# Four retention gates of a hybrid decoder, computed as one block product of seven, with the gate applied at the bank

## The chip, the core and the metric

The kernel runs on one core of one Trainium2 chip. The time is that of one execution on the device in microseconds (us); of several runs the median is taken. A profile is one further execution, recorded instruction by instruction.

The engines are named as in the profile: PE is TensorE (matmuls; PEld its weight loads), DVE is VectorE, ACT is ScalarE, POOL is GpSimd, SP is SyncE. The last two mostly start transfers here.

## What is computed

Two decoder layers over 512 tokens with 1024 channels, fp32, and a final norm. Of a layer, the part that matters:

```
h = rmsnorm(x);  z = h @ w_in        # q, k, v of attention | rq rk rv rg of retention | gate_a | gate_b
ya = sliding_window_sink_attention(aq, ak, av, sinks) @ w_a
r  = chunkwise_retention(rq, rk, rv)                        # 4 heads, 256 values each
r  = r * rsqrt(mean(r*r, axis=-1) + EPS)                    # per head
r  = r * silu(rg)                                           # rg: 1024 columns of z
yb = r @ w_b
x  = x + (sigmoid(ga) * ya + sigmoid(gb) * yb) @ w_out
x  = x + square(relu(rmsnorm(x) @ w_up)) @ w_down
```

## The kernel before

**Layout.** Activations lie with channels on the 128 partitions and tokens along the row: a tile of 128 x 512 is 128 channels of all tokens, and x is eight of these. The 1024 columns of rg are thus eight tiles `rg[0]` to `rg[7]`, two for each retention head.

**Precision.** Every fp32 operand is split into a high and a low part of a narrower kind (`split`: ScalarE writes the high part, VectorE the rest), and each product is three matmuls: high by high, high by low, low by high (`products`, lines 390 to 392).

**Weights.** `unit_order` lists all weight units, 128 x 1024 floats (512 KB) each. SyncE loads them in that order into five `raw` buffers; `split_until` splits them (line 338 on ScalarE, line 339 on VectorE) into four `hi` and four `lo` buffers, up to four units ahead of their use.

**Chunks.** `chunk("w_in", ...)` makes one tile of 128 output channels from one unit: 8 blocks of input channels by 3, so 24 matmuls with 512 columns into one of five banks of the pool `ps_mm`; a function then evacuates the bank. The retention gates come from `put_rg(i)` (line 981): times the row of inverse norms, and for i >= 4 at once `silu(i)`. The merge gate of `gate_b` comes from `gate(...)` (line 826) in tiles `gb`.

**Block products of seven.** The values of retention (`values`), the output projection (`output`) and most of the MLP multiply two-by-two blocks with seven block products instead of eight. One operand's sums are made in DRAM by GpSimd's transfers (`sum_steps`, tensors `sums_*`) and by `add_values` on VectorE (line 318); the other operand's are made on the core. For `values` these are `Turned`: the upper and lower halves of the input channels by the first and second half of the tokens (256 each). `load` fetches two `xg` tiles of x again by GpSimd's queue (line 878), `build` scales them (line 888), forms the four differences (lines 891 to 894) and splits them. `turned[1]` to `turned[4]` are the results, each four blocks of 128 x 256; `quarter(half, tokens)` gives the plain ones out of `xh`, `xl`.

**Order.** The program is traced in the order below; a scheduler then fixes each engine's queue ahead of time by a priority that follows this order and by its own estimate of when each instruction can run, so later matmuls may be pulled forward where earlier ones wait. `background` generators (attention, retention) are advanced from within chunks; `drain()` runs them to their end.

1. q, k, v of attention; eight chunks of gate_a, `qk(0)`, rg chunks 0 to 3, with attention behind them; `drain()`
2. sigmoids of gate_a, `silu` of 0 to 3, `qk(1)`, `turned.build(0)` after attention's last split, `turned.load(2)`
3. rg chunks 4 and 5
4. `w_a`: four units, eight results of 12 matmuls, each multiplied into gate_a (line 1142); `turned.build(2)` after the second unit
5. `values(turned)`, then retention of heads 0 and 1 behind `qk(2)`, `qk(3)`
6. rg chunks 6 and 7, then gate_b chunks 0 to 3, with retention of heads 2 and 3 behind them
7. `w_b` results 0 to 3 (`group`), gate_b chunks 4 to 7, `w_b` results 4 to 7, the output projection `wo`

**Retention.** `Head.scores` makes a head's decayed scores (tile `ret`), `outputs(e)` its two output tiles (bank `r` of the pool `ps_aux`, three banks): ScalarE copies the bank to `rr` (line 1044) and squares it (line 1046). `norm` makes the inverse norms, and `finish` multiplies the gate by them (line 1066), by `rr` (line 1067) and splits the result for `w_b`.

**GpSimd's queue.** `pace(tile)` counts evacuations; every second one copies a mark of one column and then issues the next step of `sum_steps`, so the sums in DRAM are spread over the layer. Between `turned.take()` and the values' first evacuation `quiet` holds it.

Of the kernel before, what the change touches and what calls it, by code (L numbers as in the profile page):

```python
# [10 lines left out]
F32 = mybir.dt.float32  # L11
F32R = mybir.dt.float32r
AF = mybir.ActivationFunctionType
ALU = mybir.AluOpType
# [28 lines left out]

N_IN = 38
N_BLOCK = 8
# [11 lines left out]
def unit_order(layer):  # L57

    order = [("w_in", i) for i in range(4 + 2 + 8 + 2 + 4 + 2 + 2)]
    order += [("w_a", i) for i in range(4)]  # L60
    order += [("rv", part, u) for part in range(7) for u in range(2)]
    order += [("w_in", i) for i in range(24, 34)]
    order += [("w_b", i) for i in range(4)]
    order += [("w_in", i) for i in range(34, 38)]
# [50 lines left out]
@with_exitstack  # L115
def decoder(ctx, tc, xT, x_first, w_in, w_rv, w_a, w_b, w_wo, w_up, w_pair, w_down, w_end, tables, decay, band, g_last, out):
    nc = tc.nc
# [62 lines left out]
    def load_until(n):  # L180
# [26 lines left out]
    sums_last = dram.tile([P, 2, UNIT], F32, name="sums_last")  # L207
    MIXING = {"rv": w_rv, "wo": w_wo}
    sums_mix = {
        name: [dram.tile([2, P, 2 * UNIT], F32, name=f"sums_{name}{l}") for l in range(DEPTH)] for name in MIXING  # L210
    }
# [102 lines left out]
    def add_values(i):  # L314
        part = order[i][2]
        if part in (2, 4):
            raws[i] = raws.pop(i - 2)
            nc.vector.tensor_tensor(raws[i], raws[i], raws.pop(i - 4), ALU.add)

# [294 lines left out]
    def layer_body(layer):  # L614
# [366 lines left out]
        def put_rg(i):  # L981
            def put(ps):
                if i % 2 == 0:
                    two = big("z")
                    rg[i], rg_next[i + 1] = two[:, 0, :], two[:, 1, :]
                else:
                    rg[i] = rg_next.pop(i)
                nc.vector.tensor_tensor(rg[i], ps, rstd(), ALU.mult)
                if i >= 4:
                    pace(rg[i])  # L990
                    silu(i)

            return put

        def silu(i):
# [12 lines left out]
        class Head:  # L1008
# [5 lines left out]
            def scores(self, js):  # L1014
# [14 lines left out]
                if js[-1] == NB - 1:  # L1029
                    slots.give(*rq.pop(h), *rk.pop(h))  # L1030
                    self.rr, self.sq = [], []

            def outputs(self, e):
# [10 lines left out]
                nc.scalar.activation(r, ps, AF.Copy)  # L1044
# [33 lines left out]
        def retention(pair):  # L1078
# [47 lines left out]
        turned.load(2)  # L1126
        for i in (4, 5):
            chunk("w_in", layer, xs, put_rg(i))


# [17 lines left out]

        load_decay(0)
        values(turned)  # L1150
        background.append(retention(0))
# [12 lines left out]

        for c in range(4):
            gate_tile(c)
            chunk("w_in", layer, xs, gate(gates[c]))
# [45 lines left out]

        TOKENS = (slice(0, H), slice(H, T))
        ms = Mixed()
# [64 lines left out]
        def output():  # L1280
# [5 lines left out]
            def multiply(ps, moving, start=True):  # L1286
                for u in range(2):
                    hi, lo = unit("wo", layer)
                    for k in range(2):
                        vh, vl = moving[2 * u + k]  # L1290
                        for n in range(4):
# [3 lines left out]
                            for w, v in ((hi, vh), (hi, vl), (lo, vh)):  # L1295
# [7 lines left out]
                                ).ins  # L1303

            def both(t):
                return t.rearrange("p (a t) -> p a t", t=H)

# [498 lines left out]
def _w_in_units(w):  # L1806
# [19 lines left out]
    units += qk(1)  # L1826
    units += _units_chunks(w, O_RG + T + r(2 * P))
    units += qk(2) + qk(3)
    units += _units_chunks(w, O_RG + T + 2 * P + r(2 * P))
    units += _units_chunks(w, O_GB + r(D))  # L1830
# [11 lines left out]
def _mixing_blocks(w):  # L1842

    blocks = []
    for u in range(2):
# [4 lines left out]
        blocks.append(np.concatenate(parts, 1))  # L1850
    return blocks


# [43 lines left out]
def _laid_out(x, g_mix, w_in, sinks, w_a, w_b, w_out, g_mlp, w_up, w_down, g_final):  # L1897
# [10 lines left out]
        "x_first": np.concatenate([sinks, gains, xT[:, 0, :]], 1),  # L1908
        "w_in": _stack(w_in, _w_in_units),
        "w_rv": _stack(w_in, lambda w: _mixing_blocks(w[:, O_RV : O_RV + D])),  # L1910
        "w_a": _stack(w_a, lambda w: _units_chunks(w[wa_rows], r(D))),
# [29 lines left out]
```

## Time and profile before

| | us |
|---|---|
| median of three runs | 1461.87 (1461.82 to 1464.63) |
| the profiled execution | 1464.35 |
| its span, first to last instruction | 1462.3 |
| TensorE busy in the span | 1450.0 |
| VectorE | 1169.0 |
| ScalarE | 969.0 |
| GpSimd | 222.3 |

TensorE's granted clock is 0.999 of full speed over the span. Matmul records overlap, since matmuls are pipelined, so what one costs is read from the distance between starts and not from its duration. A row of a group gives its count, its busy time, the mean duration in ns, and then the idle time of its engine just before it with what ended that. A row of the timeline gives start, duration, engine, line, operation and tiles.

### The profile page before, as it was taken

How to read it: one execution, taken by the hardware profiler on the slowest of the kernel's cores; microseconds unless marked ns; L12 is line 12 of the kernel's file. 1: busy time of each engine (PE TensorE's matmuls, PEld its weight loads, DVE VectorE, ACT ScalarE, POOL GpSimd, SP SyncE). 2: the span in 40 equal slices, each digit the busy share in tenths (PEclk: the TensorE clock that was granted, in tenths of full speed). 3: DMA queues.
4: the chain of work that ended last, by engine and by line, in shares of the span. 5: the costliest groups of instructions: out<-in, count | busy, mean ns of one | idle time of the engine just before them, and what ended most of it. 6: DMA issues, size and time to landing. Idle time of an engine off the chain costs nothing.

```text
span 1462.3 us, 22150 instructions
## 1 busy us (share of the span) xinstructions
PE 1450.0 (99%) x8041; PEld 1265.4 (87%) x8041; DVE 1169.0 (80%) x1762; ACT 969.0 (66%) x1592; POOL 222.3 (15%) x329
## 2 busy tenths in 40 slices
PE   9999999999999999999999999999999999999998
PEld 7888888888988999999888888888889799999997
DVE  6978876876898888888778788687778988788885
ACT  6657556543687777777756575565437777777775
POOL 0011012112101111111201110112120111111120
PEclk9999999999999999999999999999999999999999
DMA  7598369899745777666955983797885477777664
GB/s 257 177 288 225 103 174 299 232 244 255 224 119 195 192 197 190 165 184 179 307 178 172 290 222 111 217 291 219 222 210 174 137 198 201 191 192 197 178 185 146
DMA packets 96428, 297.57 MB, mean 203 GB/s; under 512 B 11328, under 2 KB 11456, under 8 KB 90432
## 3 DMA queue, kind: packets, MB, share of 16 engines
q0 software_dynamic: 35936, 125.58, 37.2%
q1 hardware_dynamic: 59664, 169.27, 33.4%
q8 instruction: 63, 1.03, 0.3%
q10 hardware_dynamic: 720, 1.31, 0.2%
q14 instruction: 45, 0.37, 0.1%
HBM read 256.54 MB, written 115.87 MB: 255 GB/s over the span
## 4 chain that ended last, share of the span: by engine, by line
PE 96%; ACT 1%; DMA 1%; DVE 1%; issue 0%; DVEq 0%; ACTq 0%
PE mm L390 23%; PE mm L391 23%; PE mm L392 23%; PE wo L1296 5%; PE b L390 3%; PE b L391 3%; PE b L392 3%; PE rv L392 2%; PE rv L390 2%; PE rv L391 2%; PE mm L405 2%; PE score L773 1%; PE pT L738 1%; PE r L392 1%; PE r L391 1%; PE r L390 1%
## 5 line engine op out<-in xcount | busy, mean ns | idle before, releaser
L338 ACT ACTIVATE hi<-raw 128x1024 fp32r<-128x1024 f32 (+1 forms) x387 | 394.1, 1021 | 263.4 <-PE mm L391 146.9
L339 DVE TENSOR_TENSOR lo<-raw,hi 128x1024 fp32r<-128x1024 f32 (+1 forms) x388 | 452.7, 1174 | 107.4 <-ACT hi L338 105.3
L390 PE MATMUL mm<-xh,hi 128*128 128x512 f32 (+1 forms) x976 | 343.8, 356 | 1.8 <-ACT xh L413 1.0
L391 PE MATMUL mm<-xl,hi 128*128 128x512 f32 (+1 forms) x976 | 344.6, 356 | 0.0
L392 PE MATMUL mm<-xh,lo 128*128 128x512 f32 (+1 forms) x976 | 340.4, 355 | 0.0
L390 PEld LDWEIGHTS mm<-xh,hi 128*128 128x128 f32 x976 | 185.2, 190 | 27.7 <-ACT xh L413 1.7
L391 PEld LDWEIGHTS mm<-xl,hi 128*128 128x128 f32 x976 | 185.3, 190 | 24.2
L392 PEld LDWEIGHTS mm<-xh,lo 128*128 128x128 f32 x976 | 183.9, 190 | 23.6
L391 PE MATMUL mm<-r,hi 128*128 128x256 f32 (+1 forms) x608 | 189.2, 311 | 0.0
L392 PE MATMUL mm<-r,lo 128*128 128x256 f32 (+1 forms) x608 | 189.0, 311 | 0.0
L390 PE MATMUL mm<-r,hi 128*128 128x256 f32 (+1 forms) x608 | 186.6, 311 | 0.5 <-ACT mm L1471 0.5
L390 PEld LDWEIGHTS mm<-r,hi 128*128 128x128 f32 x608 | 115.8, 190 | 8.8 <-ACT mm L1471 0.7
L391 PEld LDWEIGHTS mm<-r,hi 128*128 128x128 f32 x608 | 115.8, 190 | 8.0
L392 PEld LDWEIGHTS mm<-r,lo 128*128 128x128 f32 x608 | 115.8, 190 | 6.3
L1619 POOL DMA_DIRECT2D y<-eu x56 | 62.4, 1354 | 374.4 <-DVE eu L1604 373.8
L391 PE MATMUL mm<-lo,r 128*128 128x512 f32 (+1 forms) x276 | 104.3, 387 | 0.0
L392 PE MATMUL mm<-hi,r 128*128 128x512 f32 (+1 forms) x276 | 101.3, 387 | 0.0
L390 PE MATMUL mm<-hi,r 128*128 128x512 f32 (+1 forms) x276 | 98.4, 390 | 0.9 <-ACT eu L1614 0.6
L390 PE MATMUL b<-hi,r 128*128 128x512 f32 x180 | 70.5, 392 | 1.6 <-DVE eu L1604 1.2
L391 PE MATMUL b<-lo,r 128*128 128x512 f32 x180 | 70.3, 390 | 0.0
L1296 PE MATMUL wo<-r,hi 128*128 128x256 f32 x384 | 69.4, 283 | 0.0
L392 PE MATMUL b<-hi,r 128*128 128x512 f32 x180 | 67.9, 390 | 0.0
(323 smaller groups left out, 2682.5 us busy)
## 6 DMA issues: line engine op xcount, KB each, us to landing
raw<-w_in_in SPq DMA_DIRECT2D x73, 512.0 KB, 5.8
sums_down<-w_down_in POOLq DMA_DIRECT2D x30, 1024.0 KB, 11.6
sums_up<-w_pair_in POOLq DMA_DIRECT2D x56, 512.0 KB, 10.9
raw<-w_down_in SPq DMA_DIRECT2D x45, 512.0 KB, 7.6
raw<-w_pair_in SPq DMA_DIRECT2D x84, 256.0 KB, 3.7
y<-y POOLq DMA_DIRECT2D x63, 256.0 KB, 9.4
y<-eu POOLq DMA_DIRECT2D x61, 256.0 KB, 8.1
raw<-sums_down SPq DMA_DIRECT2D x30, 512.0 KB, 7.4
```

The source lines that it names most:

```text
L338: state["high"] = nc.scalar.activation(hi[:, at], raw[:, at], AF.Copy).ins
L339: nc.vector.tensor_tensor(lo[:, at], raw[:, at], f32(hi[:, at]), ALU.subtract)
L390: nc.tensor.matmul(ps, ah, bh, start=start and i == 0, stop=False, **more)
L391: nc.tensor.matmul(ps, ah, bl, start=False, stop=False, **more)
L392: latest[0] = nc.tensor.matmul(ps, al, bh, start=False, stop=stop and i == n - 1, **more).ins
L405: latest[0] = nc.tensor.matmul(ps, w[:, cols(j, c)], moving[k][low], start=first, stop=bool(final)).ins
L738: nc.tensor.transpose(pt[:, i * P : (i + 1) * P], sm[:, at : at + P], ident)
L773: nc.tensor.matmul(ps[:, g * w : (g + 1) * w], q_s[g][:, c, at], part[:, keys], start=i == 0, stop=i == 1)
L1296: latest[0] = nc.tensor.matmul(o, w[:, cols], v, start=start and first and n % 2 == 0 and w is hi and v is vh, stop=final and w is lo, ski ...
L1619: nc.gpsimd.dma_start(y[:, 2 * j + m, i * T : (i + 1) * T], t, **how)
```

## The change

Retention gates 4 to 7 (512 columns of rg) no longer come from four chunks. They are computed by `last_gates` between the `w_a` results and the values, as seven block products over the same input forms as the values. Four stay chunks. The weights' block `w_rg` has seven units, of which five are loaded, two of these from sums made in DRAM, and two are added on VectorE. In step 6 gate_b chunks 4 and 5 take the place of rg chunks 6 and 7; two gate_b chunks are left in step 7. The copy `rr` is gone: `outputs` multiplies the bank into the gate directly, and `finish` then only multiplies by the inverse norm. `retention` no longer waits for the gates.

```diff
+    order += [("rg", part, 0) for part in range(7)]
     order += [("rv", part, u) for part in range(7) for u in range(2)]
...
-        for name, at in (("rv", 0), ("wo", 14)):
-            jobs[at:at] = [(sums_mix[name][layer][u], MIXING[name][layer, u], 2 * UNIT) for u in range(2)]
+        for name, at in (("rv", 0), ("rg", 0), ("wo", 15)):
+            jobs[at:at] = [(sums_mix[name][layer][u], MIXING[name][layer, u], 2 * UNIT) for u in range(TALL[name])]
...
-                if i >= 4:
-                    pace(rg[i])
-                    silu(i)
...
+        def last_gates(turned):
+            a, b, c = (bank(ps_mm, "rg") for _ in range(3))
+            two = [big("z") for _ in range(2)]
+            def multiply(ps, moving, start=True):
+                hi, lo = unit("rg", layer)
+                for k, (vh, vl) in enumerate(moving):
+                    for n in range(2):
+                        o, cols = ps[:, n * H : (n + 1) * H], slice((2 * k + n) * P, (2 * k + n + 1) * P)
+                        for w, v in ((hi, vh), (hi, vl), (lo, vh)):
+                            nc.tensor.matmul(o, w[:, cols], v,
...
+            def keep(ps, sign):
+                t = temp("kept")
+                nc.scalar.activation(t, ps, AF.Copy, scale=float(sign))
+                return both(t)
+            def put(i, j, ps, sign, kept=None):
+                v = two[i][:, :, TOKENS[j]]
+                by = rstd()[:, TOKENS[j]].unsqueeze(1).broadcast_to([P, 2, H])
+                if kept is not None:
+                    nc.vector.scalar_tensor_tensor(kept, both(ps), float(sign), kept, ALU.mult, ALU.add)
+                    nc.vector.tensor_tensor(v, kept, by, ALU.mult)
+                else:
+                    nc.vector.scalar_tensor_tensor(v, both(ps), float(sign), by, ALU.mult, ALU.mult)
+            def done(i):
+                for m in range(2):
+                    rg[4 + 2 * i + m] = two[i][:, m, :]
+                    silu(4 + 2 * i + m)
+            multiply(a, quarter(0, 0))
+            nc.scalar.activation(b, a, AF.Copy)
+            multiply(c, turned[1])
+            five = keep(c, -1)
+            multiply(b, turned[2], False)
+            sum_two = keep(b, 1)
+            multiply(a, quarter(1, 0), False)
+            put(0, 0, a, 1)
+            multiply(c, quarter(1, 1), False)
+            put(0, 1, c, 1, sum_two)
+            done(0)
+            multiply(b, turned[3], False)
+            put(1, 1, b, -1, five)
+            multiply(b, turned[4], False)
+            put(1, 0, b, -1)
+            done(1)
...
-                if e == 0:
-                    self.both = big("rr")
-                r = self.both[:, e, :]
-                nc.scalar.activation(r, ps, AF.Copy)
                 q = temp("sq")
                 nc.scalar.activation(q, ps, AF.Square)
-                pace(r)
-                self.rr.append(r)
+                z = rg[2 * h + e]
+                nc.vector.tensor_tensor(z, ps, z, ALU.mult)
+                pace(z)
...
                     nc.vector.tensor_tensor(z, z, self.inv, ALU.mult)
-                    nc.vector.tensor_tensor(z, self.rr[e], z, ALU.mult)
+                    pace(z)
...
-            while 4 * pair + 3 not in rg:
-                yield
...
-        for i in (4, 5):
-            chunk("w_in", layer, xs, put_rg(i))
...
         load_decay(0)
+        last_gates(turned)
         values(turned)
...
-        for i in (6, 7):
-            chunk("w_in", layer, xs, put_rg(i))
...
-        for c in range(4):
+        for c in range(6):
             gate_tile(c)
             chunk("w_in", layer, xs, gate(gates[c]))
...
-        for c in range(4, KD):
+        for c in range(6, KD):
             gate_tile(c)
             chunk("w_in", layer, xs, gate(gates[c]))
```

More of the change, by code (lines that the diff above doesn't have):

```diff
@@ L42 @@
 O_GB = O_GA + D
-N_IN = 38
+N_IN = 34
 N_BLOCK = 8
@@ L57, in unit_order @@
 def unit_order(layer):
-    order = [("w_in", i) for i in range(4 + 2 + 8 + 2 + 4 + 2 + 2)]
+    order = [("w_in", i) for i in range(4 + 2 + 8 + 2 + 4 + 2)]
     order += [("w_a", i) for i in range(4)]
+    order += [("rg", part, 0) for part in range(7)]
     order += [("rv", part, u) for part in range(7) for u in range(2)]
-    order += [("w_in", i) for i in range(24, 34)]
+    order += [("w_in", i) for i in range(22, 32)]
     order += [("w_b", i) for i in range(4)]
-    order += [("w_in", i) for i in range(34, 38)]
+    order += [("w_in", i) for i in range(32, 34)]
     order += [("w_b", i) for i in range(4, 8)]
@@ L115, in decoder @@
 @with_exitstack
-def decoder(ctx, tc, xT, x_first, w_in, w_rv, w_a, w_b, w_wo, w_up, w_pair, w_down, w_end, tables, decay, band, g_last, out):
+def decoder(ctx, tc, xT, x_first, w_in, w_rg, w_rv, w_a, w_b, w_wo, w_up, w_pair, w_down, w_end, tables, decay, band, g_last, out):
     nc = tc.nc
@@ L207, in decoder @@
     sums_last = dram.tile([P, 2, UNIT], F32, name="sums_last")
-    MIXING = {"rv": w_rv, "wo": w_wo}
+    MIXING = {"rg": w_rg, "rv": w_rv, "wo": w_wo}
+    TALL = {name: w.shape[1] for name, w in MIXING.items()}
     sums_mix = {
-        name: [dram.tile([2, P, 2 * UNIT], F32, name=f"sums_{name}{l}") for l in range(DEPTH)] for name in MIXING
+        name: [dram.tile([n, P, 2 * UNIT], F32, name=f"sums_{name}{l}") for l in range(DEPTH)]
+        for name, n in TALL.items()
     }
@@ L314, in add_values @@
     def add_values(i):
-        part = order[i][2]
+        name, part = order[i][1:3]
         if part in (2, 4):
-            raws[i] = raws.pop(i - 2)
-            nc.vector.tensor_tensor(raws[i], raws[i], raws.pop(i - 4), ALU.add)
+            n = TALL[name]
+            raws[i] = raws.pop(i - n)
+            nc.vector.tensor_tensor(raws[i], raws[i], raws.pop(i - 2 * n), ALU.add)
     def split_until(n):
@@ L988, in put, with both @@
                 nc.vector.tensor_tensor(rg[i], ps, rstd(), ALU.mult)
-                if i >= 4:
-                    pace(rg[i])
-                    silu(i)
-            return put
+            return put
+        TOKENS = (slice(0, H), slice(H, T))
+        def both(t):
+            return t.rearrange("p (a t) -> p a t", t=H)
+        def last_gates(turned):
[7 more added lines that the diff above has]
+                        for w, v in ((hi, vh), (hi, vl), (lo, vh)):
+                            nc.tensor.matmul(
+                                o,
+                                w[:, cols],
+                                v,
+                                start=start and k == 0 and n == 0 and w is hi and v is vh,
+                                stop=k == 3 and n == 1 and w is lo,
+                                skip_group_check=True,
+                            )
+            def keep(ps, sign):
[30 more added lines that the diff above has]
+            done(1)
@@ L1030, in scores @@
                     slots.give(*rq.pop(h), *rk.pop(h))
-                    self.rr, self.sq = [], []
+                    self.sq = []
             def outputs(self, e):
@@ L1303, in multiply @@
                                 ).ins
-            def both(t):
-                return t.rearrange("p (a t) -> p a t", t=H)
             def keep(ps, sign):
@@ L1851, in _mixing_blocks, with _gate_block @@
     return blocks
+def _gate_block(w):
+    n = 2 * P
+    parts = []
+    for f, k in ((0, 0), (n, 0), (n, T), (0, T)):
+        parts.append(w[k : k + T, f : f + n].reshape(4, P, n).transpose(1, 0, 2).reshape(P, UNIT))
+    return [np.concatenate(parts, 1)]
 def _down_blocks(w):
@@ L1909, in _laid_out @@
         "w_in": _stack(w_in, _w_in_units),
+        "w_rg": _stack(w_in, lambda w: _gate_block(w[:, O_RG + T : O_RG + 2 * T])),
         "w_rv": _stack(w_in, lambda w: _mixing_blocks(w[:, O_RV : O_RV + D])),
```

3 lines of the change are left out of this document (removed).

## The prediction

> **What bounds the kernel now.** The page first: busy time of each engine, then the chain of work that ended last. After it the view of the waits, TensorE's only.
>
> ```profile
> PE 1450.0 (99%) x8041; PEld 1265.4 (87%) x8041; DVE 1169.0 (80%) x1762; ACT 969.0 (66%) x1592; POOL 222.3 (15%) x329
> PE 96%; ACT 1%; DMA 1%; DVE 1%; issue 0%; DVEq 0%; ACTq 0%
> PE b L390 <- DVE eu L1604: 1.2, 1, 1.2
> ```
>
> TensorE (PE) is busy 99% of the span, the chain runs 96% over it, and its longest listed wait is 1.2 us. So the time is TensorE's work plus whatever wait the change opens; work taken from other engines counts only if TensorE waited for it. VectorE (DVE), at 80%, is the next engine.
>
> The price of a matmul is its spacing, since the records overlap. The chain in order of time and the timeline give both widths; the view of one tile gives the weight load beside them.
>
> ```profile
> 872.25 0.39 PE L392 MATMUL mm<-xh,lo 128*128 128x512 f32 x1
> 884.72 0.39 PE L390 MATMUL mm<-r,hi 128*128 128x512 f32 x1
> 1090.48 34.40 PE wo L1296 x288
> L1296 PEld LDWEIGHTS wo<-r,hi x384: 187/192/193, 366.1 to 1130.9; 128*128 128x128 f32 x192
> ```
>
> Between the first two rows run 55 matmuls of 512 columns: the last 7 of `qk(1)` and the 48 of retention-gate chunks 4 and 5 (24 each; the second row is the first matmul of the `w_a` chunks). 12.47/55 = 0.2267 us each. The output projection `wo`, already a product of seven with 256-column matmuls, runs at 34.40/288 = 0.1194 us each. Two halves therefore cost 5% more than one whole, and the weight load of 0.19 us is hidden without pacing the 256-column matmuls.
>
> **TensorE's work.** Removed: 4 chunks of 24 in 2 layers, 192 x 0.2267 = 43.53 us. Added: 7 products of 4 x 2 x 3 = 24 half-width matmuls in 2 layers, 336 x 0.1194 = 40.12 us. Difference: -3.4 us. The saving of one product in eight is 12.5%, of which the narrow form takes back 5 points.
>
> [...]
>
> **What loses its cover.** Retention-gate chunks 4 and 5 stood between the end of attention and the `w_a` chunks, which read attention's last split (`r<-whole`). With them gone the `w_a` chunks come up 48 x 0.2267 = 10.9 us earlier. Timeline of layer 1 (ScalarE, then VectorE), and the same split in layer 0 with its first `w_a` matmul:
>
> ```profile
> 871.77 1.27 ACT L760 ACTIVATE whole<-pv 64x512 f32<-64x512 f32 x2 [4.15 <-PE pv L759]
> 873.06 1.15 ACT L997 ACTIVATE sig<-z 128x512 f32<-128x512 f32 x2
> 875.47 1.06 ACT L338 ACTIVATE hi<-raw 128x1024 fp32r<-128x1024 f32 x1
> 876.43 0.61 ACT L410 ACTIVATE r<-whole 128x512 fp32r<-128x512 f32 x1
> 877.82 0.69 DVE L411 TENSOR_TENSOR r<-whole,r 128x512 fp32r<-128x512 f32 x1
> 149.20 0.69 DVE L411 TENSOR_TENSOR r<-whole,r 128x512 fp32r<-128x512 f32 x1
> 160.72 0.39 PE L390 MATMUL mm<-r,hi 128*128 128x512 f32 x1
> ```
>
> Layer 0: `w_a` would come up at 160.72 - 10.88 = 149.84 and the split ends at 149.89: 0.05 us. Layer 1: 884.72 - 10.88 = 873.84 against 878.51, a hole of 4.67 us. The split stands in ScalarE's queue behind two sigmoids and a weight split, so it does not come earlier by itself. What can fill the hole is work that the scheduler already pulls forward elsewhere: retention's first scores.
>
> ```profile
> 893.10 0.39 PE L390 MATMUL ret<-late 128*128 128x512 f32 x1
> 894.32 0.39 PE L390 MATMUL mm<-r,hi 128*128 128x512 f32 x1
> ```
>
> Six such matmuls took 1.22 us, and a single filler matmul (`rv<-xh,ones`) before them 0.22. I take 1.44 us of fill, for two free banks of the small PSUM pool; the hole left is 3.2 us. Bounds: 0 if more is pulled in or the split moves ahead in the queue, 4.67 if nothing is.
>
> **The turned inputs.** The second product of the new block needs `turned[1]`. Its second load waits for a buffer that `build(0)` frees; the product before it gave cover, and the cover shrinks as well. Layer 1:
>
> ```profile
> 889.42 0.53 POOL L878 DMA_DIRECT2D xg<-spill  x1 [9.80 <-DVE r L411]
> 894.59 0.73 ACT L888 ACTIVATE xg<-xg,x 128x512 f32<-128x512 f32 x1 [1.65 <-DMA xg<-spill]
> 902.60 0.68 DVE L411 TENSOR_TENSOR r<-xg,r 128x512 fp32r<-128x512 f32 x1
> L1142 DVE TENSOR_TENSOR x<-x,mm 128x512 f32<-128x512 f32 x16 | 10.9, 684 | 4.5 <-PE mm L392 4.5
> ```
>
> Load, scaling, differences and split end at 903.28 now. TensorE would arrive at 878.51 + 96 x 0.2267 + 24 x 0.1194 = 903.14. That is level. What can make the inputs later is four `w_a` evacuations (L1142) that now queue ahead of them on VectorE, 4 x 0.684 = 2.7 us; the lower bound is 0, since the fourth product can be pulled in front. I take 0.3 us a layer, near the level pair of times: 0.6.
>
> **VectorE around it.** Windows over the retention-gate chunks 4 and 5 and the `w_a` chunks in layer 1, then in layer 0, then the `wo` stage; the first row names the columns. Below them the groups that price the added work.
>
> ```profile
> core 0: us, PE busy (x) PEld busy (x) DVE busy (x) ACT busy (x) POOL busy (x), PEclk, DMA share, GB/s
> 873.80:884.70 10.90, 10.90 (x49) 9.01 (x49) 9.57 (x15) 9.32 (x15) 0.57 (x1) 1.00 0.29 96
> 884.70:906.50 21.80, 21.80 (x98) 18.13 (x97) 20.23 (x29) 11.82 (x16) 0.53 (x1) 1.00 0.30 97
> 149.80:160.70 10.90, 10.90 (x49) 9.02 (x49) 10.12 (x16) 7.53 (x12) 0.57 (x1) 1.00 0.35 115
> 160.70:182.50 21.80, 21.80 (x98) 18.03 (x97) 18.32 (x24) 10.16 (x14) 0.53 (x1) 1.00 0.28 93
> 1090.00:1132.00 42.00, 42.00 (x351) 41.79 (x350) 37.80 (x47) 29.24 (x44) 4.44 (x9) 1.00 0.55 182
> L339 DVE TENSOR_TENSOR lo<-raw,hi 128x1024 fp32r<-128x1024 f32 (+1 forms) x388 | 452.7, 1174 | 107.4 <-ACT hi L338 105.3 <-PE wo L1296 0.5
> L318 DVE TENSOR_TENSOR raw<-raw 128x1024 f32<-128x1024 f32 x16 | 19.5, 1220 | 0.2
> L998 DVE TENSOR_TENSOR z<-z,sig 128x512 f32<-128x512 f32 x16 | 10.9, 686 | 1.0 <-ACT sig L997 0.9
> ```
>
> In layer 1 VectorE is busy 9.57 + 20.23 = 29.8 of 32.7 us here. The two chunks take away four operations (4 x 0.686 = 2.7) and two weight splits (2 x 1.174 = 2.3): 24.8. The block adds seven splits (8.2), two sums of weight parts (2.4), six evacuating operations (4.1) and four products with the sigmoid (2.7): 17.4, so 42.2 us in a stretch in which TensorE has 21.8 + 20.1 = 41.9. On paper VectorE is full. Against a loss: splits run up to four units ahead, 4 x 24 x 0.1194 = 11.5 us; the values' block behind it needs less; and the `wo` stage holds its spacing with VectorE at 37.8/42 = 90%. Cost in the sum 0, the other end is the rival below. ScalarE, at 9.32 + 11.82 = 21.1 of 32.7 us here, has room for its three extra splits.
>
> **Edits that I cost at nothing.** Retention's copy of each output goes, and its product moves from `finish` to `outputs`:
>
> ```profile
> L1044 ACT ACTIVATE rr<-r 128x512 f32<-128x512 f32 x16 | 9.6, 598 | 10.1 <-PE r L392 10.1
> sums_rv<-w_rv_in POOLq DMA_DIRECT2D x8, 1024.0 KB, 8.8
> 60.00:100.00 40.00, 40.00 (x207) 33.86 (x206) 33.24 (x111) 22.82 (x65) 7.58 (x16) 1.00 0.95 278
> ```
>
> ScalarE loses 9.6 us of copies, but no listed wait of TensorE is for them; VectorE has the same number of products, earlier. An output's bank is then freed by a VectorE product that may stand behind others; TensorE has `qk` and gate chunks to run meanwhile. If that cover failed it would be one operation, 0.7 us, per output. In the new block the seventh product adds to bank `b` as the sixth does, and waits until VectorE has read it between them; the values' first product, 24 x 0.2267 = 5.4 us, can run there, and without it the wait is again one operation and what is queued ahead. The wait for retention gates 6 and 7 in `retention` goes; merge-gate chunks 4 and 5 take the place of their chunks, so six chunks still cover the second retention. Between the `w_b` group and the last `w_b` chunks two merge-gate chunks stand instead of four. The marks that release GpSimd's queue change: four calls fewer with the gates, eight more in `finish`. That queue gets one more pair of 1 MB copies a layer at its front, 8.8 us each, and the values' copies come one step later. The stretch of the first copies has its transfers at 0.95 and TensorE busy 40.00 of 40, and the weights are wanted 100 us later: 0. SyncE loads five units instead of four: 0 for the same reason.
>
> **Sum.** -3.4 + 0.05 + 3.2 + 0.6 = +0.4 us. The profiled execution took 1464.35 us (span 1462.3); that makes 1464.8. It lies 2.5 above the median of the runs, 1461.87, so on the median's scale 1462.3.
>
> **Rivals.** *The saving stays whole.* The hole in layer 1 is filled (retention's later scores, or the fourth product) or never opens because the scheduler orders the split sooner: 1461.87 - 3.4 = 1458.5. For it: TensorE has been kept at 40.00 of 40 almost everywhere by pulled-forward work. Against it: only 7 matmuls of `qk(1)` are left there, and the units that follow `w_a` wait for weight buffers.
>
> *VectorE becomes the bound from the first `w_a` chunk to the end of the new block* (slower). Its idle share in layer 1 above is 2.9/32.7 = 9% although its queue is loaded; if it keeps that share, 42.2 us of work take 46.4, 4.5 longer than TensorE's 41.9, in each layer. That replaces the two waits in the sum: -3.4 + 9.0 = +5.6, so 1467.5; with the hole of layer 1 besides, 4.67 more at most. It decides from the point where the splits enter the block less than 4.5 us (two units) ahead. For it: in layers 0 and 1 VectorE is at 93% and 88% over the first window, so the lead is not built up there. Against it: the `wo` stage.
>
> *Half-width matmuls are paced by their weight loads* in this place, 0.19 us each: 336 x 0.19 = 63.8 instead of 40.1, +20.3 on the saving, near 1482. The `wo` row speaks against it, with the same form and width. [...]
>
> **How the numbers follow.** About 0.2%, 2.9 us, is what a measurement of this kernel can tell from no change. The forecast, between holes filled and holes open, has 0.36 and its own range is 1459.0 to 1464.8. The whole saving has 0.29; VectorE as bound or holes that add up 0.34; paced matmuls 0.01. The saving ends 3.4 below the median, hardly over the limit; a re-ordered schedule may shift another 1 us of the small waits, so the range begins at 1457.5. Upward it takes in the VectorE case with half of the unfilled hole, 1467.5 + 2.4, so 1470.0.
>
> **What would show it.** In the profile after: matmuls into a new tile `rg` at 0.119 us each (else the first term is wrong); in layer 1 a TensorE wait of some 3 us for the split of `whole` before the first `w_a` matmul, none in layer 0; a short wait or a filler before the second product; VectorE at over 95% in that stretch; no wait for `r`, for raw weights or for `sums_rg`. The prediction is wrong if TensorE's idle time does not grow, or grows elsewhere, above all between the `w_b` group and the `wo` stage, where the cover is two chunks shorter.

## The result and the profile after

| | before | after |
|---|---|---|
| median | 1461.88 us (1461.82 to 1464.63) | 1478.23 us (1476.35 to 1480.37) |
| profiled execution | 1464.35 us | 1479.34 us |
| its span | 1462.3 us | 1477.3 us |

The change makes the kernel slower: ratio 1.0101, 95% interval 1.0088 to 1.0114. The forecast was 1462.3 in a range of 1457.5 to 1470.0. The page after, engines and chain:

```profile
PE 1452.4 (98%) x8185; PEld 1272.5 (86%) x8185; DVE 1181.3 (80%) x1776; ACT 974.7 (66%) x1590; POOL 228.8 (15%) x335
PE 94%; ACT 2%; DMA 2%; issue 1%; DVE 1%; POOL 0%; DVEq 0%; ACTq 0%; POOLq 0%
```

Against the lines of before, the chain (the work that ended last, followed back) has lost two points of PE and won one each of ACT, DMA and issue: TensorE waits. The view of TensorE's waits says where (what waited for whom: us in total, times, longest):

```profile
PE wo L1348 <- DVE lo L343: 8.4, 1, 8.4
PE mm L394 <- ACT r L414: 3.0, 3, 1.7
PE mm L394 <- ACT eu L1663: 2.1, 1, 2.1
```

The new block, in the chain in order of time (start, us, what):

```profile
175.55 17.27 PE rg L1012 x144
910.65 17.27 PE rg L1012 x144
```

The block runs in both layers without a stop, 17.27/144 = 0.120 us a matmul. The longest wait before was 1.2 us; now there is one of 8.4, in the output projection of layer 0, far behind the edit.

**The account.** Take the distance of each matmul to the next one, less the usual one of its width (0.2267 and 0.120 us), and add these up by place, after minus before:

| place | us |
|---|---|
| `w_a`, layer 0 (140 to 160 us) | +2.3 |
| `w_a`, layer 1 (880 to 900) | +2.5 |
| output projection, layer 0 (380 to 400) | +10.3 |
| first MLP block, layer 1 (1160 to 1200) | +3.1 |
| all the rest | +0.1 |
| TensorE's work (336 x 0.120 - 192 x 0.2267) | -3.2 |
| sum (spans: +15.0) | +15.1 |

**The big one.** GpSimd's queue in the timeline, before and then after:

```profile
365.01 1.14 POOL L1252 DMA_DIRECT2D x<-xT_in  x2 [6.18 <-DVE r L411]
382.97 1.06 POOL L1252 DMA_DIRECT2D x<-xT_in  x2 [2.28 <-DVE r L411]
393.75 1.11 POOL L241 DMA_DIRECT2D sums_last<-sums_down  x1
405.29 0.84 POOL L242 DMA_DIRECT2D sums_last<-w_down_in  x1 [10.43 <-DMA sums_last<-sums_down]
```

```profile
357.65 1.83 POOL L242 DMA_DIRECT2D sums_last<-w_down_in  x1
373.10 1.08 POOL L244 DMA_DIRECT2D sums_last<-sums_down  x1 [9.95 <-issue]
384.09 0.83 POOL L245 DMA_DIRECT2D sums_last<-w_down_in  x1 [9.91 <-DMA sums_last<-sums_down]
384.73 3.45 POOL L1304 DMA_DIRECT2D x<-xT_in  x6
```

`x<-xT_in` reloads the residual x, whose buffers had been lent out. Before, the reloads stood ahead of the two accumulations that end layer 0's `sum_steps`; after, they stand behind them, and the queue stands still for 9.91 us, until the first accumulation has landed, before it issues the second. The first reloads leave 20 us later, at 384.73. VectorE's and TensorE's timelines after:

```profile
379.89 1.22 DVE L322 TENSOR_TENSOR raw<-raw 128x1024 f32<-128x1024 f32 x1
394.17 0.69 DVE L1370 TENSOR_TENSOR x<-x,kept 128x512 f32<-128x512 f32 x1 [13.07 <-DMA x<-xT_in]
394.78 1.22 DVE L343 TENSOR_TENSOR lo<-raw,hi 128x1024 fp32r<-128x1024 f32 x1
396.05 0.58 PE L1348 MATMUL wo<-r,lo 128*128 128x256 f32 x1 [8.41 <-DVE lo L343]
```

VectorE stood 13.07 us at the addition to x, with a weight split behind it in its queue; TensorE waited 8.41 for that split, so 4.7 us of VectorE's stand were covered by work that TensorE still had. Then the windows of TensorE's granted clock (the column PEclk):

```profile
core 0: us, PE busy (x) PEld busy (x) DVE busy (x) ACT busy (x) POOL busy (x), PEclk, DMA share, GB/s
388.00:396.00 8.00, 0.00 (x0) 0.00 (x0) 1.83 (x3) 0.00 (x0) 0.18 (x1) 0.79 0.72 217
396.00:399.00 3.00, 2.95 (x14) 2.95 (x15) 3.00 (x5) 0.09 (x1) 1.07 (x2) 0.50 0.30 63
400.00:402.00 2.00, 2.00 (x19) 2.00 (x19) 2.00 (x3) 1.86 (x2) 0.00 (x0) 1.00 0.99 358
1182.00:1184.00 2.00, 2.00 (x7) 1.52 (x6) 1.77 (x2) 0.83 (x1) 1.11 (x2) 0.50 0.57 199
```

For 3.4 us after the wait (396.05 to 399.42) TensorE had half its clock (0.50), and the 14 matmuls of 256 columns from 396.43 on came 0.213 us apart in place of 0.120. The 15 matmuls from 396.05 on took 3.37 us, and 15 x 0.120 = 1.80, so 1.6 is lost. The same came behind the 2.1 us wait in the MLP block (last row, 0.50).

One thing is needed to read the spans below. The kernel's first matmuls run slowly, for a time that differs between the profiled executions. Timelines of before, then of the first experiment:

```profile
5.84 2.08 PE L390 MATMUL mm<-xh,hi 128*128 128x512 f32 x4 [1.00 <-ACT xh L413]
7.72 1.91 PE L391 MATMUL mm<-xl,hi 128*128 128x512 f32 x4
9.43 1.16 PE L392 MATMUL mm<-xh,lo 128*128 128x512 f32 x4
10.43 0.40 PE L390 MATMUL mm<-xh,hi 128*128 128x512 f32 x1
```

```profile
5.80 1.20 PE L396 MATMUL mm<-xh,hi 128*128 128x512 f32 x4 [0.96 <-ACT xh L419]
8.65 0.39 PE L396 MATMUL mm<-xh,hi 128*128 128x512 f32 x1
```

In before, four matmuls take 1.71 us from 7.72 on, 0.43 each; at half clock in the MLP block of the changed kernel (1181.81 to 1183.94) matmuls of 512 columns are 0.43 apart too. In experiment 1 the four from 6.84 us on take 0.91, 0.23 each. That the slow start is half clock is the author's estimate from the equal spacing; it is not shown, since the windows of both executions have PEclk at 1.00 in all of the first 20 us.

The same place is reached at 10.43 or 8.65 us. The profiled before and after both have the long slow start (7 and 8 matmuls from 4 to 8 us), so their difference holds; of experiments 1 to 10 all but experiment 3 (7 matmuls) have a short one (11 to 14), and their spans are short against the one of before, in experiment 1 by 1.8 us. Ratios come from all runs.

### The profile page after: what moved, and what is told of

Its sections match the earlier page's. It is cut to its first block, busy times and chain, and to the rows that moved or that the text cites. A ratio compares the mean times of both kernels' runs of the same rounds, so it can differ in the third digit from the quotient of the medians.

```text
span 1477.3 us, 22469 instructions
## 1 busy us (share of the span) xinstructions
PE 1452.4 (98%) x8185; PEld 1272.5 (86%) x8185; DVE 1181.3 (80%) x1776; ACT 974.7 (66%) x1590; POOL 228.8 (15%) x335
## 4 chain that ended last, share of the span: by engine, by line
PE 94%; ACT 2%; DMA 2%; issue 1%; DVE 1%; POOL 0%; DVEq 0%; ACTq 0%; POOLq 0%
PE mm L395 22%; PE mm L394 22%; PE mm L396 22%; PE wo L1348 4%; PE rg L1012 3%; PE b L394 3%; PE b L395 3%; PE b L396 3%; PE rv L395 2%; PE rv L394 2%; PE rv L396 2%; PE mm L409 2%; PE score L777 1%; PE pT L742 1%; DMA sums_last<-sums_down 1%
## 5 line engine op out<-in xcount | busy, mean ns | idle before, releaser
L342 ACT ACTIVATE hi<-raw 128x1024 fp32r<-128x1024 f32 (+1 forms) x393 | 400.3, 1022 | 256.7 <-PE mm L395 127.4
L343 DVE TENSOR_TENSOR lo<-raw,hi 128x1024 fp32r<-128x1024 f32 (+1 forms) x394 | 459.1, 1173 | 94.5 <-ACT hi L342 91.4
L394 PE MATMUL mm<-xh,hi 128*128 128x512 f32 (+1 forms) x912 | 319.1, 354 | 1.5 <-ACT xh L417 0.7
L395 PE MATMUL mm<-xl,hi 128*128 128x512 f32 (+1 forms) x912 | 319.6, 353 | 0.0
L396 PE MATMUL mm<-xh,lo 128*128 128x512 f32 (+1 forms) x912 | 316.2, 353 | 0.0
L394 PEld LDWEIGHTS mm<-xh,hi 128*128 128x128 f32 x912 | 173.2, 190 | 25.2 <-ACT xh L417 1.4
L395 PEld LDWEIGHTS mm<-xl,hi 128*128 128x128 f32 x912 | 173.3, 190 | 22.0
L396 PEld LDWEIGHTS mm<-xh,lo 128*128 128x128 f32 x912 | 172.3, 190 | 21.2
L394 PE MATMUL b<-hi,r 128*128 128x512 f32 x180 | 70.8, 393 | 1.2 <-DVE eu L1653 1.2
L283 DVE TENSOR_TENSOR raw<-raw 128x512 f32<-128x512 f32 x56 | 38.4, 686 | 41.2 <-DMA raw<-w_pair_in 34.8
```

Of the source, the lines that this page charges most:

```text
L283: nc.vector.tensor_tensor(raws[i][:, at], last[:, LEFT], last[:, RIGHT], ALU.add)
L342: state["high"] = nc.scalar.activation(hi[:, at], raw[:, at], AF.Copy).ins
L343: nc.vector.tensor_tensor(lo[:, at], raw[:, at], f32(hi[:, at]), ALU.subtract)
L394: nc.tensor.matmul(ps, ah, bh, start=start and i == 0, stop=False, **more)
L395: nc.tensor.matmul(ps, ah, bl, start=False, stop=False, **more)
L396: latest[0] = nc.tensor.matmul(ps, al, bh, start=False, stop=stop and i == n - 1, **more).ins
```

## Experiments

Two theories to begin with. Q: the order on GpSimd's queue makes the 8.4 us. W: the earlier `w_a` makes the other waits. All ratios are to the kernel before, run on the same chip.

**1. Two empty steps.** The changed kernel, with the accumulations two steps later:

```
         if whole == N_BLOCK:
             ...
+            yield
+            yield
             nc.gpsimd.dma_start(sums_last, r11...)
```

> The changed kernel with two empty steps ahead of the sums_last transfers in layer 0's sum_steps, so that GpSimd's queue has the eight reloads of x (x<-xT_in) ahead of the sums_last accumulations again, as before the change; all else is as changed. Theory Q (queue order: the extra marks let the sums_last steps, which wait for one another, pass the reload; the reload lands late, VectorE stands at x<-x,kept and the weight splits behind it, and the output projection of layer 0 waits): the 8.4 us wait of the output projection goes, about 9 to 11 us less than the changed kernel, 1467 to 1469. Rival D (transfers: the retention weights' sums and loads crowd the transfers around the reload): the wait stays, 1476 to 1480. Rival C (cover: two merge-gate chunks fewer stand between the w_b group and the output projection, so TensorE arrives before the reload in any order): most of the wait stays, over 1474.

1468.56 us, ratio 1.0035 (1.0025 to 1.0044). GpSimd's queue:

```profile
363.82 1.14 POOL L1306 DMA_DIRECT2D x<-xT_in  x2 [5.74 <-DVE r L417]
390.67 1.10 POOL L246 DMA_DIRECT2D sums_last<-sums_down  x1
```

and TensorE's waits, from the first:

```profile
PE mm L396 <- ACT r L416: 3.0, 3, 1.7
PE mm L396 <- ACT eu L1665: 2.1, 1, 2.1
```

The wait of `wo` is gone and 9.7 us of the change's 16.4 with it. Nothing else was touched: that the position of these steps makes the 8.4 us is shown. Its rivals, crowded transfers and too little cover, would have kept the wait; both fall. The two other waits stay.

**2. The marks alone, on the kernel before.** `finish` gets one mark for each of its four heads, four in a layer, as many as the change adds on balance (the expectations of runs 6 and 8 call them eight by mistake):

```
     nc.vector.tensor_tensor(z, self.rr[e], z, ALU.mult)
+    if e:
+        pace(z)
```

> The kernel before with one mark more per head in finish (after its second split), and nothing else of the change. In GpSimd's queue the sums_last accumulations then stand ahead of the reload of x, as in the changed kernel. Theory Q: a wait of the output projection in layer 0 appears, 1465 to 1473 depending on how late the accumulations' sources are. Rivals D and C: within 2 us of the kernel before.

1466.34 us, 1.0023 (1.0010 to 1.0036). The timeline, and the longest of TensorE's waits:

```profile
369.42 0.84 POOL L242 DMA_DIRECT2D sums_last<-w_down_in  x1 [8.92 <-DMA sums_last<-sums_down]
369.95 2.53 POOL L1254 DMA_DIRECT2D x<-xT_in  x4
381.31 0.69 DVE L1323 TENSOR_TENSOR x<-x,kept 128x512 f32<-128x512 f32 x1 [0.79 <-DMA x<-xT_in]
```

```profile
PE ret L390 <- DVE s L1027: 2.0, 1, 2.0
```

A miss in the place. The order is that of the changed kernel, yet VectorE waits 0.8 us and `wo` not at all; the profile shows a wait of retention instead. The chain of accumulations ended 15 us earlier here (369.4 against 384.1); the changed kernel has one sum more ahead of it in each layer. So Q had to become: order, and a chain that ends after VectorE wants x at some 381 us.

**3. The cover alone.** The kernel before, with retention-gate chunks 4 and 5 (and their weights in `unit_order`) behind `w_a`.

> The kernel before with retention-gate chunks 4 and 5 behind the w_a results in place of ahead of them; the same instructions, and the reload's place in the queue unchanged. Theory W (the two chunks were the cover between attention's last split and w_a): a wait of about 1.8 us before the first w_a matmul in each layer, as in the changed kernel, 1464.5 to 1466.5. Rival (the wait before w_a comes from the new block's demands on VectorE and ScalarE): no wait there, 1461 to 1463.

1467.05 us, 1.0023 (1.0013 to 1.0032). The longest of TensorE's waits:

```profile
PE mm L391 <- ACT r L411: 1.8, 2, 1.7
```

Layer 1 waits as in the changed kernel. Layer 0 does not: there 27 matmuls of `qk(1)` were left behind attention's last product, in the changed kernel only 9. So W is shown for layer 1. Half of the forecast missed: it had a wait in both layers, and the time lies 0.5 us above its range. The 18 matmuls that are missing in layer 0 (18 x 0.2267 = 4.1 us) are more than the wait there, so another order of the fill is enough to explain it; why the scheduler orders it so was not taken apart.

**4. The first product as cover.** Experiment 1, with the block's first product, which reads x as it stands, ahead of `w_a`:

```
+    order += [("rg", 0, 0)]
     order += [("w_a", i) for i in range(4)]
-    order += [("rg", part, 0) for part in range(7)]
+    order += [("rg", part, 0) for part in range(1, 7)]
...
+    gates_of = last_gates(turned)      # a generator that yields after its first product
+    next(gates_of)
     aT = ...                           # w_a
-    last_gates(turned)
+    next(gates_of, None)
```

> The kernel of the two empty steps, with the new block's first product (plain inputs, its weight unit moved ahead of w_a's in the order of loads) ahead of the w_a results as cover. Theory W: 24 x 0.12 = 2.9 us of work stand in the two waits of 1.8 and 2.3 us before w_a, so 3 to 4 us less than with the two empty steps alone, 1463 to 1466. If the waits only move behind w_a (the turned inputs' second load is late), no more than 1 us less.

1463.91 us, 1.0001 (0.9992 to 1.0011). The longest of TensorE's waits, and its timeline in layer 0:

```profile
PE rv L397 <- ACT hi L345: 2.1, 2, 1.0
```

```profile
182.84 0.28 PE L1014 MATMUL rg<-r,lo 128*128 128x256 f32 x1
184.15 0.73 PE L397 MATMUL rv<-hi,xh 128*128 128x512 f32 x2 [1.03 <-ACT hi L345]
```

The waits before `w_a` are gone in both layers, and the one of the MLP block too, though nothing was edited there: it comes and goes with the order that the scheduler makes. That makes the gain 4.7 us, more than the 3 to 4 forecast from the waits before `w_a` alone. New is a wait of 1.0 us in each layer inside the block (1.2 by the spacing of the matmuls).

**5. Fifth and sixth product swapped,** in experiment 4 (`turned[3]` into bank b before `quarter(1, 1)` into bank c, weights likewise), to part the two products that add into b.

> The previous kernel (two empty steps, first product ahead of w_a; span 1460.4 us) with the new block's fifth and sixth products in the other order, so that the last product, which adds into the same bank as the sixth did, has another product between itself and the VectorE step that reads that bank. Theory A (the 1.2 us stands in front of the seventh product in each layer come from this hand-over: TensorE had taken a matmul of the values' first product meanwhile, whose split was not there yet): both go, PE rv <- ACT hi loses its 2.1 us, and the time is 1461 to 1462 us, 2 us under the previous one, level with the kernel before or 1 us under it. Theory B (ScalarE and VectorE are late there whatever the order, because the block asks for seven splits in 20 us): the stands move to the next product and the time stays at 1463 to 1464 us.

1463.26 us, 1.0003 (0.9995 to 1.0012); the same 2.1 us. Theory A fell: the wait stood not at the hand-over between sixth and seventh product but behind the first four products (96 matmuls), ahead of the fifth, as it had in experiment 4. The swap itself was hardly tested: the scheduler ran 22 of the 24 matmuls of `quarter(1, 1)` ahead of the product with `turned[3]` again.

**6. A later chain, on experiment 2:** one empty step ahead of the copy into `sums_last`.

> The kernel before with eight more marks in each layer, as in the run before_marks, and one empty step ahead of the copy that opens the sums_last chain: the accumulations stay ahead of the reload of x on GpSimd's queue, but the chain opens one step later. Theory Q (order and lateness together: VectorE stands at x<-x,kept from the point at which the second accumulation's issue, some 10 us after the first, falls behind VectorE's own arrival there at about 380 us): in the run before_marks the reload's issue began at 370.0 and x was waited for 0.8 us; with the chain a step (some 15 us) later the reload's issue falls to 380 to 386, VectorE stands 8 to 14 us, TensorE shows wo <- DVE lo of 3 to 9 us, time 1469 to 1476 us. If lateness does not matter (rival: the wait in the changed kernel needs its other splits in that stage too): no wait in wo, 1463 to 1468 us.

1466.34 us, 1.0023 (1.0012 to 1.0033). Inconclusive: the chain became only 2 us later (second accumulation at 371.45), VectorE waited 0.6 us. The size of the delay was misjudged, so it says nothing for or against.

**7. The second half of the change alone,** on the kernel before: products out of PSUM in `outputs`, no copy `rr`, the gates awaited ahead of the outputs.

> The second half of the change alone on the kernel before: retention's outputs are multiplied with their gate out of PSUM, the copy into rr is gone, the mark stays on the product (no added marks in finish), retention waits for its gates ahead of its outputs. Queue order of the reload of x as in the kernel before. Theory (this half is worth nothing by itself, 16 copies of ScalarE less off the path): 1461 to 1465 us, within 0.2% of the kernel before, PE waits as in before within 1 us. Rival (the outputs' bank stays longer on VectorE, or the rg chunks 6 and 7 come too late for the outputs): waits of ret or of r appear, 2 to 5 us more.

1462.51 us, 0.9998 (0.9989 to 1.0007), longest waits 1.2 and 1.1 us as before. Alone, on the kernel before, this half is worth nothing and costs nothing.

**8 and 10. One and two links more.** Experiment 2, with one copy, then two, behind the last accumulation, each waiting for the transfer before:

```
     nc.gpsimd.dma_start(sums_last[:, 1, :], r12, accum_op=ALU.add)
+    nc.gpsimd.dma_start(sums_more, sums_last[:, 1, :])
+    nc.gpsimd.dma_start(sums_most, sums_more)      # the second link, run 10 only
```

> The run before_marks (the kernel before with eight more marks in each layer, the accumulations ahead of the reload of x) with one more link at the end of its chain: a copy of half of sums_last to a place that nobody reads, which must wait for the last accumulation, and stands ahead of the reload on GpSimd's queue. Theory Q (order, and a chain that ends after VectorE wants x at some 380 us): the links of that chain are 10 us apart, so the reload, issued from 370 us on in before_marks, now begins at 379 to 382 us; VectorE stands 5 to 12 us at x<-x,kept, TensorE shows wo <- DVE lo of 2 to 8 us around 385 to 395 us, and the time is 1468 to 1475 us. Rival (the wait needs the changed kernel's other splits in that stage; a late reload alone is taken up by the splits that are already done): VectorE stands, but no wait of wo over 1 us, 1463 to 1468 us.

> The run one_link_more with a second copy after the first (from the one place that nobody reads to another), which waits for it and stands ahead of the reload of x too. In one_link_more the reload's issue began at 377.9 us, VectorE stood 2.8 us at x<-x,kept and TensorE did not wait; in the changed kernel it began at 384.7 us, VectorE stood 13.1 us and TensorE 8.4 us, so some 4.7 us of VectorE's stand were covered. Theory Q, with that cover: the second copy holds the queue 6 to 8 us more, the reload begins at 384 to 386 us, VectorE stands 9 to 13 us, TensorE shows wo <- DVE lo of 4 to 8 us near 390 us, and the time is 1470 to 1475 us. Rival (the wait in wo needs the changed kernel's other splits): VectorE stands 9 us or more and no wait of wo over 1 us, 1464 to 1468 us.

One link: 1466.13 us, 1.0030 (1.0015 to 1.0045); two: 1470.78, 1.0055 (1.0039 to 1.0072). GpSimd's and VectorE's rows with one link; then GpSimd, VectorE, TensorE with two:

```profile
377.87 2.18 POOL L1256 DMA_DIRECT2D x<-xT_in  x4 [0.16 <-issue]
385.23 0.69 DVE L1325 TENSOR_TENSOR x<-x,kept 128x512 f32<-128x512 f32 x1 [2.81 <-DMA x<-xT_in]
```

```profile
383.26 0.51 POOL L246 DMA_DIRECT2D sums_most<-sums_more  x1 [3.94 <-DMA sums_more<-sums_last]
383.91 3.23 POOL L1258 DMA_DIRECT2D x<-xT_in  x6
392.53 0.69 DVE L1327 TENSOR_TENSOR x<-x,kept 128x512 f32<-128x512 f32 x1 [10.01 <-DMA x<-xT_in]
394.41 0.58 PE L1302 MATMUL wo<-r,lo 128*128 128x256 f32 x1 [5.36 <-DVE lo L343]
```

With one link the forecast of Q missed: the reload came 1 us earlier than expected, VectorE's 2.8 us were covered, TensorE did not wait, and the time is in the rival's range. With two the wait of the changed kernel is there, on a kernel that has nothing of its new block: 10.0 us of VectorE, 5.4 of TensorE, and the cover is 4.6 against 4.7. (The profiled execution is the slowest of the four, 1474.38 us against 1470.55 to 1470.96, with half clock behind this wait, 0.50 from 394 to 398 us, and behind one of 2.2 us in retention, 0.59 from 272 to 276, so the typical wait may be shorter.) That settles Q: order alone makes no wait (experiment 2), lateness with the reload ahead makes none (experiment 1, accumulation at 390.67), and the two together do, with and without the new block.

**9. The change without its marks in `finish`.** In this kernel the marks run out too soon, so layer 0's last accumulations come after those weights were loaded: its last MLP block multiplies with an unfinished sum (loaded from 693 us on, accumulated at 775 and 787). Each engine runs as many instructions as in the changed kernel.

> The changed kernel without the mark that its finish adds for each head's two products (eight calls of pace fewer in each layer), nothing else. Theory Q: the reload of x stands ahead of the accumulations on GpSimd's queue again, VectorE doesn't wait for it over 2 us, wo <- DVE lo goes from TensorE's waits, and the time is that of the run with two empty steps, 1466 to 1471 us. Rival (the one more sum job and the changed order of the splits make the wait, not the marks): wo <- DVE lo of 5 us or more stays, 1474 to 1480 us.

1471.45 us, 1.0065 (1.0050 to 1.0080). The reload leaves at 363.60 and `wo` does not wait, as Q says; the time, 0.5 us above the forecast, holds the waits of experiment 1, half clock behind that of `eu` (0.57 from 1172 to 1176 us), and 3.2 us for `r<-qlo` in layer 1's attention. So it is the marks that move the accumulations ahead of the reload, but some of them are needed to finish the sums in time.

**11 and 12. ScalarE's order.** In experiment 4 ScalarE had three weight splits queued ahead of the copies `kept`, one of which frees the bank of the fifth product. Run 11 issues each later split after those copies; run 12 also takes the product with `quarter(1, 0)` as second, ahead of the turned ones.

```
+    copied = []
     def multiply(ps, moving, start=True):
+        with ExitStack() as queue:
+            for ins in copied:
+                queue.enter_context(tc.issue_after(ins))
             hi, lo = unit("rg", layer)
...
-    nc.scalar.activation(t, ps, AF.Copy, scale=float(sign))
+    copied.append(nc.scalar.activation(t, ps, AF.Copy, scale=float(sign)).ins)
```

> The run first_product (two empty steps, the first product ahead of w_a) with ScalarE's order changed in the new block: the weight splits of each later product are issued after the copies (kept) of the products before. There, ScalarE issued three splits ahead of the two copies, the fifth product adds into the bank that the first copy reads, and TensorE stood 1.2 us in each layer. Theory C (the copies behind the splits make that stand): rv <- ACT hi of 2.1 us goes from TensorE's waits, and the time falls by 2 to 2.7 us against the run first_product, to 1461 to 1462 us, 0.1 to 0.2% under the kernel before. Rival (the splits that now come later are missed instead): TensorE waits 1 us or more in each layer for a split of rg or rv, and the time stays at 1463 to 1465 us.

> The run copies_first with the block's second product over the values' input as it stands (the fourth before), the two over turned inputs behind it, so that the turned inputs have 2.9 us more. Theory C: as in copies_first, 1461 to 1462 us; if there the two products over turned inputs still waited for their last operand (in the run first_product they were issued in pieces around the other one), this one is up to 0.5 us better. Rival (the order of the weights moves a sum of two units ahead of its need and VectorE is late for it): TensorE waits 1 us or more for a split of rg, 1463 to 1465 us.

Run 11: 1465.43 us, 1.0018 (1.0009 to 1.0026); run 12: 1461.69, 0.9989 (0.9980 to 0.9998). TensorE's waits in 11, then in 12:

```profile
PE mm L397 <- ACT eu L1675: 2.1, 1, 2.1
PE rg L1019 <- ACT kept L1030: 1.4, 2, 0.7
```

```profile
PE mm L397 <- ACT xh L420: 1.6, 1, 1.6
PE rg L1019 <- ACT kept L1030: 1.4, 2, 0.7
```

In both the waits inside the block fall from 2.1 to 1.4 us, now for the copy itself. Theory C is half right. Run 11 missed, at 1.5 us more than experiment 4 in place of 2 less, because the 2.1 us in the MLP block came back (layer 1, <- `eu`), some 250 us behind the edited block. Run 12 does not have it (its 1.6 us is one wait at the start) and is the only version with the new block whose ratio lies under 1, by 0.1% and hardly clear of noise: of the 3.2 us of work saved, some half remains. Why `eu` is late in the changed kernel and in runs 1, 9 and 11, and not in 4, 5 and 12, stays open; no run took it apart.

## Why the prediction was wrong, point by point

**TensorE's work, -3.4: right, -3.2 measured.** 0.120 us a matmul against 0.1194 used. The rivals of paced matmuls and of VectorE as bound did not happen: no wait stands in the block.

**The cover of `w_a`: mechanism right, sizes off.** Layer 1: 3.2 forecast, 2.5 measured; the fill was the one named (`ret` six times and `rv<-xh,ones`). Layer 0: 0.05 forecast, 2.3 measured. The step took the start of `w_a` from the old timeline, but the fill behind attention was ordered anew: 9 matmuls of `qk(1)` were left there, 27 where the chunks alone were moved (experiment 3).

**The turned inputs, 0.6: measured 0 in the changed kernel. VectorE around it, 0: right, on a load that was too high.** The step had 42.2 us of VectorE's work in 41.9, and over 95% busy as a sign to look for. From the first `w_a` matmul to the end of the block in layer 1 VectorE was busy 34.9 of 40.0 us, 87%, and in the block alone 80%. Up to here the sum would have been -3.2 + 2.3 + 2.5 = +1.6 instead of +0.4, within the range.

**"Edits that I cost at nothing": the step that failed.** Of the marks it says "four calls fewer with the gates, eight more in `finish`", and costs the queue at 0 because the sums are wanted 100 us later. It asked when the queue's transfers are wanted, not what else stands in that queue. The reload of x does; a step that moved up past it, with an issue that waits 10 us for the transfer before, cost 10.3 us with the half clock behind the wait; the step had 0. Rows of before that would have shown it were there: the reloads at 365.01 to 382.97, the accumulation next in the queue at 393.75 and the 10.43 us beside the next one. The last sentence of the prediction comes near the place, "between the `w_b` group and the `wo` stage", by luck: the wait stands 20 us inside the `wo` stage (first matmul at 367.1 us), and in experiment 1, with the same two chunks as cover, it is gone.

**What no step had:** 3.1 us in layer 1's first MLP block: a wait for `eu` of 2.1 us (0.6 before) that comes and goes with the scheduler's order, and the half clock behind it. The second half of the change is worth 0 by itself (experiment 7), as forecast.

## What to carry to other kernels

When an edit changes how many steps are released on a queue, list everything that the queue issues near the steps that move, and who waits for each, above all where an issue itself waits for an earlier transfer. A saving of 3 us on a full engine is smaller than what a new order of the instructions costs or gives, so price the edit with the new order's waits, and try small re-orderings of the same edit before judging it: here they span 1461.7 to 1478.2 us. A wait of TensorE costs more than its length where the clock falls behind it, here 1.6 us more, behind one of 8.41 us and behind one of 2.1; the next section has waits of some 2 us with and without it.

## What the runs showed of the hardware

Half the clock behind a wait: 3.4 us of it after 8.41 us without a matmul (396.05 to 399.42 us). A wait of 2.1 us was enough in the changed kernel at 1177 us, and one of 2.12 us in experiment 6, behind which the matmuls of 512 columns from 274.07 to 277.06 us are 0.43 apart in place of 0.23 (timeline, then the window):

```profile
272.44 0.33 PE L391 MATMUL ret<-r 128*128 128x128 f32 x1 [2.12 <-DVE s L1028]
```

```profile
272.00:276.00 4.00, 3.56 (x13) 2.94 (x14) 4.00 (x7) 1.43 (x3) 0.00 (x0) 0.75 0.39 115
```

The equal waits of experiments 1 (2.1 us) and 2 (2.0) left the clock at 1.00: in experiment 1 from 1164 to 1180 us, in experiment 2 from 268 to 280. The 4 us with the wait for `eu` and the next 4, in the changed kernel, then in experiments 1 and 9:

```profile
1176.00:1180.00 4.00, 1.90 (x13) 1.48 (x12) 4.00 (x6) 4.00 (x7) 1.61 (x3) 1.00 0.54 181
1180.00:1184.00 4.00, 4.00 (x13) 3.10 (x13) 3.77 (x5) 2.83 (x5) 1.44 (x2) 0.64 0.60 214
```

```profile
1164.00:1168.00 4.00, 1.89 (x13) 1.44 (x12) 4.00 (x6) 4.00 (x7) 1.53 (x3) 1.00 0.55 182
1168.00:1172.00 4.00, 4.00 (x18) 3.31 (x19) 3.77 (x5) 3.98 (x6) 1.47 (x3) 1.00 0.59 212
```

```profile
1168.00:1172.00 4.00, 1.89 (x13) 1.47 (x12) 4.00 (x6) 4.00 (x8) 1.60 (x3) 1.00 0.59 189
1172.00:1176.00 4.00, 4.00 (x12) 3.12 (x11) 3.54 (x5) 2.62 (x5) 1.17 (x2) 0.57 0.57 206
```

TensorE is busy 1.90, 1.89 and 1.89 us of the 4 with the wait, and the clock behind it is 0.64, 1.00 and 0.57. So in these runs the length of a wait of some 2 us does not tell whether half clock follows, nor does TensorE's work in the 4 us around it; what does, no run takes apart. Where it followed in the changed kernel, the matmuls from 1181.05 to 1184.69 us took 3.64 us, and 9 x 0.2267 = 2.04, so 1.6 is lost there too. Why the slow start is over by 6.84 us in experiment 1 and not by 9.43 in before, no run takes apart either.
